# A two-layer SSD and S5 encoder on one core: other buffers, another PSUM tag and another order in the second layer

## The chip, the cores and the metric

The kernel runs on 1 core of one Trainium2 chip. A time is the device time of one execution in microseconds (us); of several runs the median is given. Durations and start times are read from the profile of one execution.

## What is computed

A trunk of two layers over 512 tokens of width 1024. The part that the change touches is the mixer:

```python
proj = h @ w_in
z = proj[..., :o1]
xbc = proj[..., o1:o2]
dt_raw = proj[..., o2:o3]
u = proj[..., o3:]
xbc = jax.nn.silu(depthwise_conv_centred(xbc, conv_w, conv_b))
...
y = y_fwd + y_bwd + ssd_d[:, None] * xh
y = y.reshape(bsz, l, SSD_WIDTH) * jax.nn.silu(z)
y_ssd = rms_norm(y, ssd_norm_w)
y5 = s5_bidirectional(u, ...)
g = jax.nn.gelu(y5)
y_s5 = rms_norm(g * jax.nn.sigmoid(g @ w_glu + b_glu), s5_norm_w)
return jnp.concatenate([y_ssd, y_s5], axis=-1) @ w_out
```

`y_fwd` and `y_bwd` are chunked state-space scans with 16 heads of 64 channels in 4 groups and a state of 128 (the SSD half); `s5_bidirectional` runs 64 groups of 16 channels through a complex diagonal state of 64, forward and backward (the S5 half). A layer norm follows, then `relu(h @ w1)**2 @ w2` and another layer norm.

## The kernel before

**Staging.** The layers run one after the other. Every product of activations with a weight is made as three fp32r matmuls (high part by high part, low by high, high by low: L105 to L107). For that ACT rounds each weight tile to its high part `whi` (L94) and DVE subtracts it to get `wlo` (L95); the raw tile is loaded by SP into one of two `raw` buffers.

**The mixer** of a layer consists of two generators. `s5_stream` makes the eight u tiles, then the V stage (L406, eight units, into the tile XV), then 62 steps of a scan on the 64 chunks, three DVE operations each (L423, L426, L427) and a copy back into XV by ACT (L428), then eight y units Y0 to Y7. A y unit loads its tables Gt, U and Wy through SP, multiplies them on PE (L527, L534) into one or two PSUM banks of the tag s5, and ACT takes them out with gelu (L539, tile gs). After every second unit PE transposes gs (L546, tile gT_ps), and the result goes to DRAM, to come back as gF for the glu product.

`ssd_group` runs four times. It makes the conv tiles B and C, and then for each of two head pairs (ct, 0 to 7 in all): the conv tile x (projection `xbc_ps`, L561 to L566), its transposition Xrow (L572), the products xd (L607), the states `st_ps` (L615) and S (L621, L630); then for each of the two heads the tile R (L653), the decay sums `D_ps` on PE (L661 to L664), their exponential E (L665), the weights w (L670 to L672), E times w (L674) and the tile eb (loaded by SP, multiplied at L675 and L676); then `y_ps` on PE (L685), the skip term (L694), the gate z (a projection, silu at L698, product at L699). Finished y tiles of the first three groups wait in DRAM.

**Order.** The table `KN["mrg"][l]` has 40 numbers, one for each step of `ssd_group` (10 for each group): so many steps of `s5_stream` are written ahead of that step. S5's step 13 ends the V stage, 44 the scan, 53 the last y unit. The list of instructions then goes through a scheduler, which orders each engine's queue by priority; `KN["po"][l]` shifts the priority of named pieces (a positive number is earlier): "yo" is y_ps, "y" the y units of S5, "cv" the conv tiles B and C, "wo" the output projection. Nothing in the code has the name "wp". Each engine then works through its queue in order.

**Buffers.** `KN["sb"][l]` gives the buffers of E, eb, R, w, tmp (w2 and z) and X (Xrow). PSUM has three banks of the tag mm, one of ss, two of sm and two of s5. `D_ps` has the tag sm, with `st_ps`, Xrow's, Brow's and others; v_ps, the y units and the glu product have s5.

**After both generators** the SSD half is finished: `rms_start` makes the tile ssq in the buffer of the tag "w"; `y_split` makes of each of the eight y tiles a high and a low part (L878, L879) and adds its squares to ssq (L710, L712, L714); `rms_ps` (L719) and r_ssd (L721) follow. Then half 0 of the output projection (`rp`, 192 matmuls on up to four accumulators; taken out at L907 with r_ssd), then glu, half 1, layer norm and MLP. In the order, half 0 is interleaved with the y units of S5.

Of the kernel before, what the change touches and what calls it, by code (L numbers as in the profile page):

```python
# [10 lines left out]
F32 = mybir.dt.float32  # L11
# [31 lines left out]
KN = dict(  # L43
    mrg=[[5, 0, 1, 0, 3, 6, 3, 5, 0, 5, 4, 3, 1, 0, 0, 0, 0, 0, 8, 0,
# [3 lines left out]
    pt0=3, lag=[1, 4], vb=(3, 2), gvb=(3, 2), cbb=2, wyb=4, raw=2, whi=3, wlo=3,  # L48
    nb=dict(mm=3, ss=1, sm=2, s5=2),
    po=[{"z": -100, "v": -30, "w": 150, "scan": -60, "R": -100, "y": -30, "dt": 300, "wp": 60, "wo": 30, "yo": 30}, {"w": -300, "dt": 300, "z": -150, "R": -30, "yo": 30, "wo": 30, "wp": 15, "cv": 100}],  # L50
    sb=[{"E": 3, "eb": 2, "R": 1, "w": 1, "tmp": 2, "X": 1}, {"E": 4, "eb": 4, "R": 1, "w": 1, "tmp": 3, "X": 2}],
    ybk=[1, 2], gt=["s5", "sm"], pwt=["sm", "sm"], stpe=[0, 0], curb=2, Dt="sm", gen="212002000222332121110000",
)


# [1 line left out]
def kernel(ctx: ExitStack, tc: tile.TileContext, A, out, depth=L):  # L57
    nc = tc.nc
    V, G, S, PE = nc.vector, nc.gpsimd, nc.scalar, nc.tensor
    per = ctx.enter_context(tc.tile_pool(name="per", bufs=1))  # L60
    wp = ctx.enter_context(tc.tile_pool(name="wp", bufs=3))
# [10 lines left out]
    def psum(tag, name, cols=512):  # L72
        return ps.tile([128, cols], F32, tag=tag, name=name, bufs=NB[tag], padded_shape=[128, 512])
# [504 lines left out]
    def ssd_group(l, pool, act, prm, dtp, g, yd, ys):  # L578
# [18 lines left out]
        for j in range(2):  # L597
# [3 lines left out]
            X, Xp = to_rows(pool, xT, "Xrow", KN["sb"][l]["X"])  # L601

            St = []
            for dd in range(2):
                c0 = dd
                xd = pool.tile([128, 3, 2, 64], F32, tag="xd", name="xd", bufs=1)
                V.tensor_tensor(xd, Xp[:, c0:c0 + 3].rearrange("p c (h q) -> p c h q", h=2),  # L607
                                dtp["dec"][:, c0:c0 + 3, dd, 2 * ct:2 * ct + 2].unsqueeze(3).to_broadcast([128, 3, 2, 64]),
                                op=ALU.mult)
                sp_ = psum("sm", "st_ps")  # L610
                order = [0, 1, 2] if dd == 0 else [2, 1, 0]
                on_pe = KN["stpe"][l]

                def state(i, alone):
                    PE.matmul(sp_[:, i * 128:(i + 1) * 128], lhsT=B[:, c0 + i],  # L615
                              rhs=xd[:, i].rearrange("p h q -> p (h q)"), start=True, stop=alone)
                for i in order:
                    if i == order[0] or not on_pe:
                        state(i, True)
                s_ = pool.tile([128, 3, 128], F32, tag="S", name="S", bufs=3)  # L620
                S.activation(s_[:, order[0]], sp_[:, order[0] * 128:order[0] * 128 + 128], AF.Copy)  # L621
                for a_, b_ in ((order[0], order[1]), (order[1], order[2])):
                    if on_pe:
                        ts = pool.tile([128, 128], F32, tag="ts", name="ts", bufs=2)
                    for h in range(2):
                        hs, tot = slice(h * 64, h * 64 + 64), dtp["tot"][:, b_ + dd, dd, 2 * ct + h:2 * ct + h + 1]
                        if on_pe:
                            S.activation(ts[:, hs], s_[:, a_, hs], AF.Copy, scale=tot)
                        else:
                            V.scalar_tensor_tensor(s_[:, b_, hs], s_[:, a_, hs], tot,  # L630
                                                   sp_[:, b_ * 128 + h * 64:b_ * 128 + h * 64 + 64],
                                                   op0=ALU.mult, op1=ALU.add)
                    if on_pe:
                        state(b_, False)
                        PE.matmul(sp_[:, b_ * 128:b_ * 128 + 128], lhsT=ident, rhs=ts, start=False, stop=True)
                        S.activation(s_[:, b_], sp_[:, b_ * 128:b_ * 128 + 128], AF.Copy)
                St.append(s_)
# [3 lines left out]
            for h in range(2):  # L641
                hh = 2 * ct + h
                E = pool.tile([128, T], F32, tag="E", name="E", bufs=KN["sb"][l]["E"])
                R = pool.tile([128, 2, 8, 64], F32R, tag="R", name="R", bufs=KN["sb"][l]["R"])
                eb = pool.tile([128, 2, 384], F32, tag="eb", name="eb", bufs=KN["sb"][l]["eb"])
# [5 lines left out]
                with prio("R"):  # L651
# [1 line left out]
                    V.tensor_tensor(R, cst[:, 384:512].rearrange("p (d t) -> p d t", d=2).unsqueeze(2).to_broadcast(  # L653
                        [128, 2, 8, 64]), av.rearrange("p x c d -> p d (x c)").bitcast(F32).unsqueeze(3).to_broadcast(
                        [128, 2, 8, 64]), op=ALU.mult)
                    Dp = psum(KN["Dt"], "D_ps")
                    Dv = Dp.rearrange("p (c t) -> p c t", c=4)
                    one = [av[:, x, :, d].unsqueeze(2).to_broadcast([128, 4, 64]) for x, d in ((1, 1), (0, 0))]
                    for x in range(2):
# [33 lines left out]
            y = xT  # L693
# [11 lines left out]
    def rms_start(pool, tag):  # L705
        return pool.tile([128, T], F32, tag=tag, name="ssq", bufs=1)
# [91 lines left out]
    for l in range(depth):  # L798
# [67 lines left out]
        with pool_("sd%d" % l) as pool:  # L866
# [4 lines left out]
                next(ssd, None)  # L871
            for _ in ssd:
                pass
            rms = rms_start(pool, "w")
            yT = new_hT()

            def y_split(k, y, first):
# [33 lines left out]
        with pool_("mo%d" % l, side="right") as pool:  # L911
            hT = new_hT()
            gb = load_gb(pool, 1 + 2 * l)
            with pool_("gl%d" % l, side="right") as gl:
# [9 lines left out]
                rms = rms_start(gl, "ssq")  # L924
# [174 lines left out]
```

## Time and profile before

| | us |
|---|---|
| median of 3 runs | 1854.35 |
| lowest and highest run | 1852.96, 1860.39 |
| the profiled execution | 1860.12 |
| its span in the profile | 1858.3 |
| PE busy | 1702.1 |
| DVE busy | 1269.6 |
| ACT busy | 762.8 |
| first V matmul of layer 2 (L406) | at 1048.0 |
| first scan step of layer 2 (L423) | at 1105.39 |
| first y matmul with Wy (L534) | at 1305.28 |
| first glu matmul | at 1398.85 |

Times in the lower part count from the start of the span. PE is TensorE's matmul queue, PEld its weight loads, which overlap; DVE is VectorE, ACT ScalarE, POOL GpSimd, SP the engine that issues most DMAs. PEclk is the granted clock of TensorE as a share of full speed. A wait is idle time of an engine and what ended it; "issue" is idle time for which the profile shows no releaser. Records of neighbouring matmuls overlap, so the pace of a chain of matmuls is the distance of their starts, not their duration.

### The profile page before, as it was taken

Reading aid. Unit: us, or ns where it says so; the run is one execution under the profiler, and the core shown is the slowest. Engines: PE = TensorE matmul, PEld = TensorE weight load, DVE = VectorE, ACT = ScalarE, POOL = GpSimd, SP = SyncE. Lnnn points to the kernel's source line nnn. Section 1 sums busy time; section 2 is a strip of 40 time slices with the busy share of each in tenths; the row PEclk is TensorE's granted clock in tenths of the full one; section 3 lists DMA queues with packets and bytes.
Section 4 is the critical chain, followed back from the end, with each engine's and each line's share of the span. In section 5 each row is a group of like instructions: output and inputs, shape, how many; then the busy total and the mean of one; then the engine's idle time right before and its main releaser. Section 6 shows DMA issues by size and latency. Waiting matters only on the chain.

```text
span 1858.3 us, 27757 instructions
## 1 busy us (share of the span) xinstructions
PE 1702.1 (92%) x11068; PEld 1384.9 (75%) x11068; DVE 1269.6 (68%) x2142; ACT 762.8 (41%) x1306; POOL 72.9 (4%) x101
## 2 busy tenths in 40 slices
PE   4999988769799999999999999886889999999998
PEld 3677766657578877777888887775677888888886
DVE  7579999996646989995347659999316663434346
ACT  3235557752144432323233556667315342313231
POOL 1000000000000101110001000000000000000001
PEclk9789989779899999999999999997899999999999
DMA  5767433144534287764334875230783323223232
GB/s 192 201 173 198 114 104 98 32 141 118 141 100 125 68 254 265 266 220 136 105 104 157 232 207 157 82 99 23 222 266 114 114 82 99 92 91 102 90 100 83
DMA packets 112049, 258.70 MB, mean 139 GB/s; under 512 B 10928, under 2 KB 54832, under 8 KB 111280
## 3 DMA queue, kind: packets, MB, share of 16 engines
q1 hardware_dynamic: 104432, 230.84, 41.4%
q0 software_dynamic: 7488, 26.09, 3.9%
q8 instruction: 87, 1.43, 0.3%
q14 instruction: 42, 0.34, 0.1%
HBM read 220.19 MB, written 36.70 MB: 138 GB/s over the span
## 4 chain that ended last, share of the span: by engine, by line
PE 69%; DVE 15%; DMA 8%; issue 4%; ACT 3%; SPq 0%; POOL 0%; POOLq 0%; DVEq 0%; ACTq 0%
PE rp L105 8%; PE rp L106 8%; PE rp L107 8%; PE up_ps L105 5%; PE up_ps L106 5%; PE up_ps L107 5%; PE xbc_ps L106 2%; PE xbc_ps L105 2%; PE xbc_ps L107 2%; PE v_ps L406 2%; DVE wlo L95 2%; PE y L534 2%; PE y_ps L685 2%; PE glu_ps L106 2%; PE glu_ps L105 2%
## 5 line engine op out<-in xcount | busy, mean ns | idle before, releaser
L95 DVE TENSOR_TENSOR wlo<-raw,whi 128x1024 fp32r<-128x1024 f32 x224 | 274.5, 1226 | 313.5 <-ACT whi L94 309.0
L94 ACT ACTIVATE whi<-raw 128x1024 fp32r<-128x1024 f32 x224 | 236.9, 1059 | 523.6 <-PE up_ps L106 170.0
L105 PE MATMUL up_ps<-hThi,whi 128*128 128x512 f32 (+1 forms) x560 | 208.1, 374 | 3.3 <-DVE hr L964 3.1
L106 PE MATMUL up_ps<-hTlo,whi 128*128 128x512 f32 (+1 forms) x560 | 208.6, 373 | 0.1
L107 PE MATMUL up_ps<-hThi,wlo 128*128 128x512 f32 (+1 forms) x560 | 208.2, 372 | 0.0
L106 PE MATMUL rp<-wlo,ahi 128*128 128x512 f32 x448 | 176.9, 395 | 0.4 <-DVE wlo L95 0.4
L107 PE MATMUL rp<-whi,alo 128*128 128x512 f32 x448 | 176.5, 395 | 0.0
L105 PE MATMUL rp<-whi,ahi 128*128 128x512 f32 x448 | 165.5, 397 | 1.6 <-ACT whi L94 1.6
L105 PEld LDWEIGHTS up_ps<-hThi,whi 128*128 128x128 f32 x560 | 105.0, 188 | 23.8 <-issue 2.4
L106 PEld LDWEIGHTS up_ps<-hTlo,whi 128*128 128x128 f32 x560 | 105.5, 188 | 18.8 <-issue 0.4
L107 PEld LDWEIGHTS up_ps<-hThi,wlo 128*128 128x128 f32 x560 | 105.5, 188 | 18.7 <-issue 0.4
L105 PE MATMUL xbc_ps<-hThi,whi 128*128 128x512 f32 x256 | 104.3, 413 | 7.6 <-ACT w L671 2.6
L106 PE MATMUL xbc_ps<-hTlo,whi 128*128 128x512 f32 x256 | 103.2, 409 | 0.0
L107 PE MATMUL xbc_ps<-hThi,wlo 128*128 128x512 f32 x256 | 103.1, 408 | 0.0
L105 PEld LDWEIGHTS rp<-whi,ahi 128*128 128x128 f32 x448 | 84.0, 188 | 22.5 <-ACT whi L94 2.5
L106 PEld LDWEIGHTS rp<-wlo,ahi 128*128 128x128 f32 x448 | 84.1, 188 | 20.8 <-DVE wlo L95 0.7
L107 PEld LDWEIGHTS rp<-whi,alo 128*128 128x128 f32 x448 | 84.1, 188 | 20.8 <-issue 0.2
L428 ACT ACTIVATE XV<-cur 128x128 f32<-128x128 f32 x124 | 52.4, 427 | 63.2 <-DVE cur L427 62.9
L974 DVE TENSOR_TENSOR h<-h,rp 128x512 f32<-128x512 f32 x64 | 43.8, 690 | 49.4 <-PE rp L107 49.4
L105 PE MATMUL u_ps<-hThi,whi 128*128 128x256 f32 (+1 forms) x176 | 61.0, 355 | 5.2 <-ACT whi L94 3.3
L685 PE MATMUL y_ps<-E,Xrow 128*64 128x128 f32 x256 | 49.6, 329 | 17.3 <-DVE E L674 17.3
L105 PEld LDWEIGHTS xbc_ps<-hThi,whi 128*128 128x128 f32 x256 | 49.8, 195 | 19.6 <-ACT z L698 3.2
(291 smaller groups left out, 3737.1 us busy)
## 6 DMA issues: line engine op xcount, KB each, us to landing
raw<-in_w SPq DMA_DIRECT2D x128, 512.0 KB, 3.6
raw<-in_wi SPq DMA_DIRECT2D x64, 512.0 KB, 3.7
Pv<-pd SPq DMA_DIRECT2D x32, 512.0 KB, 6.5
raw<-in_wo SPq DMA_DIRECT2D x32, 512.0 KB, 3.6
eb<-ad SPq DMA_DIRECT2D x64, 192.0 KB, 4.4
Bv<-in_bb SPq DMA_DIRECT2D x16, 512.0 KB, 5.7
U<-Ud SPq DMA_DIRECT2D x16, 512.0 KB, 5.9
Gt<-KKd SPq DMA_DIRECT2D x128, 64.0 KB, 3.1
```

The costliest lines, as they stand in the source:

```text
L94: S.activation(hi, raw, AF.Copy)
L95: V.tensor_tensor(lo, raw, hi.bitcast(F32), op=ALU.subtract)
L105: PE.matmul(o, lhsT=sh, rhs=mh, start=first, stop=False)
L106: PE.matmul(o, lhsT=sh, rhs=ml, start=False, stop=False)
L107: PE.matmul(o, lhsT=sl, rhs=mh, start=False, stop=last)
L406: PE.matmul(pv[64 * a:64 * a + 64, ri, q], lhsT=W[:, ri, g * 64:(g + 1) * 64], rhs=U[:, g, m % 2], start=True, stop=True, tile_position=(0 ...
L428: S.activation(x1, new, AF.Copy)
L534: PE.matmul(yv[b][64 * r:64 * r + 64, q], lhsT=XV[64 * a:64 * a + 64, ri, 4 * m + p, 64 * dd:64 * dd + 64], rhs=W[dd][64 * a:64 * a + 64, ...
L685: PE.matmul(yp[64 * h:64 * h + 64, c * 128:(c + 1) * 128], lhsT=lhsT[:, 64 * h:64 * h + 64], rhs=rhs[h], start=start, stop=stop, tile_posi ...
L974: V.tensor_tensor(hs, hs, o, op=ALU.add)
```

## The change

The entry of layer 2 (the second one) in four tables is new, E, eb and X get fewer buffers and R, w and xd more. `D_ps` of layer 2 takes its PSUM bank from the tag s5. In both layers ssq takes the buffer of the tag "CBU" (one of the two masked products of C and B, read at L670) instead of that of "w". The buffers of xd and S become entries of the table; for S and for layer 1 the numbers are those from before. No arithmetic is changed. The new table has one line more, so that each line of the changed kernel has a number one higher than here: L423 becomes L424, and so on.

```diff
--- before.py
+++ after.py
@@ -43,13 +43,14 @@
 KN = dict(
     mrg=[[5, 0, 1, 0, 3, 6, 3, 5, 0, 5, 4, 3, 1, 0, 0, 0, 0, 0, 8, 0,
           0, 1, 0, 0, 0, 0, 0, 0, 1, 0, 0, 0, 1, 1, 0, 0, 0, 2, 0, 2],
-         [3, 0, 2, 1, 0, 6, 9, 1, 5, 0, 0, 0, 0, 5, 0, 0, 0, 0, 1, 0,
-          0, 0, 1, 0, 0, 0, 0, 0, 2, 0, 3, 1, 0, 3, 0, 0, 1, 0, 0, 4]],
+         [3, 6, 3, 1, 0, 0, 4, 1, 5, 0, 5, 0, 3, 4, 1, 0, 0, 0, 1, 0,
+          0, 0, 0, 0, 0, 0, 0, 0, 2, 0, 3, 0, 1, 3, 0, 3, 0, 0, 0, 2]],
     pt0=3, lag=[1, 4], vb=(3, 2), gvb=(3, 2), cbb=2, wyb=4, raw=2, whi=3, wlo=3,
     nb=dict(mm=3, ss=1, sm=2, s5=2),
-    po=[{"z": -100, "v": -30, "w": 150, "scan": -60, "R": -100, "y": -30, "dt": 300, "wp": 60, "wo": 30, "yo": 30}, {"w": -300, "dt": 300, "z": -150, "R": -30, "yo": 30, "wo": 30, "wp": 15, "cv": 100}],
-    sb=[{"E": 3, "eb": 2, "R": 1, "w": 1, "tmp": 2, "X": 1}, {"E": 4, "eb": 4, "R": 1, "w": 1, "tmp": 3, "X": 2}],
-    ybk=[1, 2], gt=["s5", "sm"], pwt=["sm", "sm"], stpe=[0, 0], curb=2, Dt="sm", gen="212002000222332121110000",
+    po=[{"z": -100, "v": -30, "w": 150, "scan": -60, "R": -100, "y": -30, "dt": 300, "wp": 60, "wo": 30, "yo": 30}, {"w": -300, "dt": 300, "z": -150, "R": -30, "yo": -30, "wo": 30, "wp": 100, "cv": 100, "y": 150}],
+    sb=[{"E": 3, "eb": 2, "R": 1, "w": 1, "tmp": 2, "X": 1, "xd": 1, "S": 3}, {"E": 3, "eb": 2, "R": 2, "w": 2, "tmp": 3, "X": 1, "xd": 2, "S": 3}],
+    ybk=[1, 2], gt=["s5", "sm"], pwt=["sm", "sm"], stpe=[0, 0], curb=2, Dt=["sm", "s5"],
+    gen="212002000222332121110000",
 )
 
 
@@ -603,7 +604,7 @@
             St = []
             for dd in range(2):
                 c0 = dd
-                xd = pool.tile([128, 3, 2, 64], F32, tag="xd", name="xd", bufs=1)
+                xd = pool.tile([128, 3, 2, 64], F32, tag="xd", name="xd", bufs=KN["sb"][l]["xd"])
                 V.tensor_tensor(xd, Xp[:, c0:c0 + 3].rearrange("p c (h q) -> p c h q", h=2),
                                 dtp["dec"][:, c0:c0 + 3, dd, 2 * ct:2 * ct + 2].unsqueeze(3).to_broadcast([128, 3, 2, 64]),
                                 op=ALU.mult)
@@ -617,7 +618,7 @@
                 for i in order:
                     if i == order[0] or not on_pe:
                         state(i, True)
-                s_ = pool.tile([128, 3, 128], F32, tag="S", name="S", bufs=3)
+                s_ = pool.tile([128, 3, 128], F32, tag="S", name="S", bufs=KN["sb"][l]["S"])
                 S.activation(s_[:, order[0]], sp_[:, order[0] * 128:order[0] * 128 + 128], AF.Copy)
                 for a_, b_ in ((order[0], order[1]), (order[1], order[2])):
                     if on_pe:
@@ -653,7 +654,7 @@
                     V.tensor_tensor(R, cst[:, 384:512].rearrange("p (d t) -> p d t", d=2).unsqueeze(2).to_broadcast(
                         [128, 2, 8, 64]), av.rearrange("p x c d -> p d (x c)").bitcast(F32).unsqueeze(3).to_broadcast(
                         [128, 2, 8, 64]), op=ALU.mult)
-                    Dp = psum(KN["Dt"], "D_ps")
+                    Dp = psum(KN["Dt"][l], "D_ps")
                     Dv = Dp.rearrange("p (c t) -> p c t", c=4)
                     one = [av[:, x, :, d].unsqueeze(2).to_broadcast([128, 4, 64]) for x, d in ((1, 1), (0, 0))]
                     for x in range(2):
@@ -871,7 +872,7 @@
                 next(ssd, None)
             for _ in ssd:
                 pass
-            rms = rms_start(pool, "w")
+            rms = rms_start(pool, "CBU")
             yT = new_hT()
 
             def y_split(k, y, first):
```

The V stage of layer 2 is now written to its end by the fourth SSD step (before: by the seventh), and two or more y units lie before the last steps of the pairs 6 and 7. The rows below are the queues of single engines, in order, in layer 2's mixer.

DVE at the end of the scan (sc and cur are the scan's tiles, ssq the sum of squares of y). Before:

```order
L427 TENSOR_TENSOR cur<-sc_11576,sc_11575 128x128
L714 TENSOR_TENSOR ssq<-ssq,yl 128x512
L423 TENSOR_TENSOR sc_11694<-cur,l_5694 128x256
L714 TENSOR_TENSOR ssq<-ssq,yl 128x512
L426 TENSOR_TENSOR sc_11695<-sc_11694,XV 128x128
L427 TENSOR_TENSOR cur<-sc_11695,sc_11694 128x128
L423 TENSOR_TENSOR sc_11701<-cur,l_5694 128x256
L426 TENSOR_TENSOR sc_11702<-sc_11701,XV 128x128
L427 TENSOR_TENSOR cur<-sc_11702,sc_11701 128x128
L694 SCALAR_TENSOR_TENSOR xbc<-xbc,sp,y_ps 128x512
L879 SCALAR_TENSOR_TENSOR hTlo<-yl,sp,hThi 128x512 x2
L699 TENSOR_TENSOR xbc<-xbc,z 128x512
```

and with the change:

```order
L428 TENSOR_TENSOR cur<-sc_11583,sc_11582 128x128
L424 TENSOR_TENSOR sc_11589<-cur,l_5694 128x256
L427 TENSOR_TENSOR sc_11590<-sc_11589,XV 128x128
L428 TENSOR_TENSOR cur<-sc_11590,sc_11589 128x128
L654 TENSOR_TENSOR R<-cst,aT 128x1024
L675 TENSOR_TENSOR E<-E,w 128x512
L654 TENSOR_TENSOR R<-cst,aT 128x1024
L675 TENSOR_TENSOR E<-E,w 128x512
L673 TENSOR_TENSOR w<-w,w_12063 128x512
L673 TENSOR_TENSOR w<-w,w_12091 128x512
L713 COPY ssq<-yl 128x512
L715 TENSOR_TENSOR ssq<-ssq,yl 128x512 x3
```

The scan's last steps had ssq work between them, which now stands behind the scan, after R and E of the last two pairs.

ACT from the end of the scan to the second y unit (XV is the copy back of a scan step, gs the gelu of a y unit; y_11874 and y_11875 are the two halves of Y0 before, y_11616 and y_11617 those after, y_11750 and y_11751 Y1). Before:

```order
L428 ACTIVATE XV<-cur 128x64x2 x4
L878 ACTIVATE hThi<-yl,sp 128x512 x2
L428 ACTIVATE XV<-cur 128x64x2
L94 ACTIVATE whi<-raw 128x1024
L710 ACTIVATE yl<-yl 128x512 x2
L878 ACTIVATE hThi<-xbc,sp 128x512
L710 ACTIVATE xbc<-xbc 128x512
L94 ACTIVATE whi<-raw 128x1024
L539 ACT_TABLE_LOAD
L539 ACTIVATE gs<-y_11874 128x2x8x16
L539 ACTIVATE gs<-y_11875 128x2x8x16
L94 ACTIVATE whi<-raw 128x1024
```

and with the change:

```order
L429 ACTIVATE XV<-cur 128x64x2 x21
L540 ACT_TABLE_LOAD
L540 ACTIVATE gs<-y_11616 128x2x8x16
L540 ACTIVATE gs<-y_11617 128x2x8x16
L666 ACT_TABLE_LOAD
L666 ACTIVATE E<-D_ps 128x512 x2
L671 ACTIVATE w<-CBU,fac 128x128 x8
L699 ACT_TABLE_LOAD
L699 ACTIVATE z<-z_ps 128x512
L540 ACT_TABLE_LOAD
L540 ACTIVATE gs<-y_11750 128x2x8x16
L540 ACTIVATE gs<-y_11751 128x2x8x16
```

21 copies of the scan follow each other, and between gs of Y0 and gs of Y1 there are now E and w of a pair and z, with table loads.

PE from the last transposition of S5 (gT_ps) to the first glu matmuls. Before:

```order
L105 MATMUL rp_12621<-whi,hThi 128x512
L546 MATMUL gT_ps<-cst,gs 128x128 x8
L106 MATMUL rp_12621<-wlo,hThi 128x512
L107 MATMUL rp_12621<-whi,hTlo 128x512
L105 MATMUL rp_12621<-whi,hThi 128x512
L106 MATMUL rp_12621<-wlo,hThi 128x512
L107 MATMUL rp_12621<-whi,hTlo 128x512
L105 MATMUL glu_ps<-ahi,whi 128x512 x2
L106 MATMUL glu_ps<-alo,whi 128x512
L107 MATMUL glu_ps<-ahi,wlo 128x512
```

and with the change (between the two pieces stand 57 more rp matmuls):

```order
L106 MATMUL rp_12618<-whi,hThi 128x512
L547 MATMUL gT_ps<-cst,gs 128x128 x8
L107 MATMUL rp_12618<-wlo,hThi 128x512
L108 MATMUL rp_12618<-whi,hTlo 128x512
L106 MATMUL rp_12619<-whi,hThi 128x512
...
L106 MATMUL rp_12621<-whi,hThi 128x512
L107 MATMUL rp_12621<-wlo,hThi 128x512
L108 MATMUL rp_12621<-whi,hTlo 128x512
L106 MATMUL glu_ps<-ahi,whi 128x512
L107 MATMUL glu_ps<-alo,whi 128x512
L107 MATMUL rp_12618<-wlo,hThi 128x512
L108 MATMUL rp_12618<-whi,hTlo 128x512
```

Behind that transposition 5 rp matmuls stood before glu; now 62 do, and 24 more are mixed with glu's.

## Rows read from the trace of the kernel before

**Rows 1.** Page: engines' busy time and share; chain that ended last, by engine.
```profile
PE 1702.1 (92%) x11068; PEld 1384.9 (75%) x11068; DVE 1269.6 (68%) x2142; ACT 762.8 (41%) x1306; POOL 72.9 (4%) x101
...
PE 69%; DVE 15%; DMA 8%; issue 4%; ACT 3%; SPq 0%; POOL 0%; POOLq 0%; DVEq 0%; ACTq 0%
```

**Rows 2.** Windows: length, busy PE, PEld, DVE, ACT, POOL, then PEclk, DMA share, GB/s.
```profile
1050.00:1100.00 50.00, 48.85 (x585) 41.07 (x582) 24.59 (x40) 26.65 (x52) 1.77 (x2) 1.00 0.80 249
1150.00:1200.00 50.00, 43.53 (x239) 36.42 (x238) 48.38 (x106) 33.07 (x71) 0.00 (x0) 0.93 0.31 90
1250.00:1300.00 50.00, 34.60 (x226) 29.02 (x226) 46.36 (x108) 37.45 (x84) 0.00 (x0) 0.79 0.11 31
1350.00:1400.00 50.00, 44.21 (x450) 34.55 (x448) 11.23 (x13) 12.19 (x22) 1.62 (x3) 0.93 0.81 239
```

**Rows 3.** Groups on DVE, 1105 to 1304 us: busy us, mean ns, idle before.
```profile
L95 DVE TENSOR_TENSOR wlo<-raw,whi 128x1024 fp32r<-128x1024 f32 x17 | 20.7, 1218 | 0.0
...
L653 DVE TENSOR_TENSOR R<-cst,aT 128x1024 fp32r<-128x1024 f32 x13 | 15.9, 1220 | 0.7 <-PE D_ps L664 0.7
L630 DVE SCALAR_TENSOR_TENSOR S<-S,fac,st_ps 128x64 f32<-128x64 f32 x56 | 13.4, 278 | 0.3 <-ACT S L621 0.2
...
L714 DVE TENSOR_TENSOR ssq<-ssq,yl 128x512 f32<-128x512 f32 x3 | 2.0, 679 | 0.0
```

**Rows 4.** Waits of DVE, 1105 to 1304 us: total, times, longest.
```profile
DVE E L674 <- ACT E L665: 2.0, 3, 1.3
...
DVE eb L675 <- DMA eb<-ad: 0.5, 1, 0.5
```

**Rows 5.** Timeline of DVE, start and end of the scan: start, duration, line.
```profile
1105.39 0.41 DVE L423 TENSOR_TENSOR sc<-cur,l 128x256 f32<-128x256 f32 x1
...
1107.11 0.42 DVE L423 TENSOR_TENSOR sc<-cur,l 128x256 f32<-128x256 f32 x1
...
1108.31 0.43 DVE L423 TENSOR_TENSOR sc<-cur,l 128x256 f32<-128x256 f32 x1
...
1300.02 0.68 DVE L714 TENSOR_TENSOR ssq<-ssq,yl 128x512 f32<-128x512 f32 x1
1300.62 0.41 DVE L423 TENSOR_TENSOR sc<-cur,l 128x256 f32<-128x256 f32 x1
...
1303.30 0.29 DVE L427 TENSOR_TENSOR cur<-sc,sc 128x128 f32<-128x128 f32 x1
```

**Rows 6.** Windows, instructions of tile y_ps alone (columns: PE busy first, PEclk).
```profile
1258.00:1266.00 8.00, 2.40 (x38) 2.16 (x38) 0.00 (x0) 1.00 0.20 30
1294.00:1304.00 10.00, 4.93 (x40) 4.32 (x40) 0.49 (x1) 0.66 0.26 75
```

**Rows 7.** Waits of PE, 1304 to 1400 us: total, times, longest.
```profile
PE y L527 <- issue: 5.6, 1, 5.6
PE y L527 <- DMA Gt<-KKd: 3.5, 1, 3.5
...
PE y L527 <- DMA U<-Ud: 1.6, 1, 1.6
```

**Rows 8.** Line L539, whole span: duration min/median/max, first and last start.
```profile
L539 ACT ACTIVATE gs<-y x24: 365/384/602, 429.7 to 1391.8; 128x256 f32<-128x256 f32 x16, 128x512 f32<-128x512 f32 x8
L539 ACT ACT_TABLE_LOAD  x2: 1283/1283/1283, 424.7 to 1313.3; - x2
```

**Rows 9.** Timeline of PE: first L534, two rp, first glu.
```profile
1305.28 1.10 PE L534 MATMUL y<-Wy,XV 64*64 64x128 f32 x32 [2.30 <-issue]
...
1318.62 0.39 PE L107 MATMUL rp<-whi,hTlo 128*128 128x512 f32 x1
1318.85 0.40 PE L105 MATMUL rp<-whi,hThi 128*128 128x512 f32 x1
...
1398.85 0.73 PE L105 MATMUL glu_ps<-ahi,whi 128*128 128x512 f32 x2 [0.39 <-ACT ahi L921]
```

**Rows 10.** Page: DMA issues of eb; KB each, median us to landing.
```profile
eb<-ad SPq DMA_DIRECT2D x64, 192.0 KB, 4.4
```

## The prediction

> **What bounds the kernel now.** I read the engine table and the chain of the page first, then windows over layer 2's mixer, then the groups and waits of single engines in two stretches of it, then single rows. Over the whole span PE is busy 92% and carries 69% of the chain that ended last, DVE 15% [rows 1]: a change of order can only win time in which PE stands still or runs at a low clock. The windows show where that is. From 1050 to 1100 PE has 48.9 of 50 us busy; from 1150 to 1200 it has 43.5 and DVE 48.4; from 1250 to 1300 PE is down to 34.6, its granted clock to 0.79, and DVE still at 46.4 [rows 2]. The last two lie in the scan stage: the 62 scan steps (L423, L426, L427) run on DVE from 1105.39 to 1303.30 [rows 3, 5], 198 us, between the DVE work of the SSD pairs, and DVE waits in it for hardly anything (the largest wait is 2.0 us in all) [rows 4]. The first y unit of S5 needs the whole scan. After it PE is the busy one again (44.2 of 50 from 1350 to 1400) and DVE almost free (11.2) [rows 2]; this is the tail, from the first L534 at 1305.3 to the first glu matmul at 1398.9, 93.6 us [rows 9]. Its PE waits are few and long: 2.3 us ahead of the first L534 [rows 9], and before single L527 5.6 us of issue, 3.5 us for Gt and 1.6 us for U [rows 7], 13.0 us together.
>
> So three terms set what a new order of the same work does: when the scan can start (PE's V stage), how long DVE takes from its first to its last step, and how long PE takes from there to glu. Counted in the two orders, every engine issues the same compute work; only order, buffers and waits differ. Outside layer 2's mixer the orders are the same but for a few places at the end of layer 1's, which I count as nothing: the last scan step and the first y unit keep their places there.
>
> **Term 1, scan start.** Ahead of the last V unit the new order holds 20 y_ps, 12 D_ps and 4 projection matmuls fewer. A set of 20 y_ps took 2.40 us at clock 1.00 [rows 6]; a projection matmul starts every 0.23 us [rows 9], and a D_ps, with half the columns, I put at 0.114. That is 2.4 + 1.4 + 0.9 = 4.7 us less on a PE that is full there [rows 2]. The V weights then have to come in closer together, which can give some of it back; bounds 0 and -4.7, taken -4.
>
> **Term 2, the scan stage on DVE.** Between first L423 and last L427 the new order holds eight L630 fewer (0.278 us, 2.2), two L653 (1.22, 2.4), one L95 more (1.22) and, net, nine others of 512 columns or less fewer (L607, L672, L674, L694 and the like, with three conv ops more), which I take at the 0.68 of an L714 (6.1): -9.5 us [rows 3]. Neighbours that do not depend on each other overlap: the 0.68 us L714 that starts at 1300.02 is followed after 0.60, so each op costs 0.08 less than its duration; with 18 ops fewer that takes back 1.4. Ops that depend on each other do not overlap: a bare scan step takes 1.20 us (1107.11 to 1108.31), which is 0.04 us per op more than its durations [rows 5]. The new order has 22 more such neighbours (before ACT's 21 XV copies in a row DVE has nothing else to interleave), 22 x 0.12 = +2.6. So far -5.5.
> On top come waits that the trace of before cannot show, those for buffers. eb goes from four to two buffers. The next pair's eb can then be loaded only after y_ps of the last pair has read the old one, and a load takes 4.4 us from issue to landing [rows 10]. With four buffers DVE waited 0.5 us for it in the whole stage [rows 4]. By the new DVE order and the durations of this trace, the first eb product of the next pair stands 7.4, 5.9, 3.4, 1.7 and 2.6 us of DVE work behind the last pair's L694, which itself follows y_ps. If L694 came at once after y_ps, 1.0 + 2.7 + 1.8 = 5.5 us would be uncovered; if DVE's backlog keeps L694 2.7 us behind, nothing. Bounds 0 and +5.5, taken +1.5, as DVE is the late engine there. E from four to three and X from two to one are read by the same y_ps; the cover is the same backlog, and the term above holds them. R, w and xd go from one to two, which can only remove waits; DVE's largest is the 2.0 us for ACT's E, which these buffers do not touch [rows 4], so I take nothing for it. Term 2: -4 (bounds -7 and +1).
>
> **Term 3, the tail.** What was in front of the first y unit and now stands behind it on PE: D_ps (24) and y_ps (40) of pairs 6 and 7, six st_ps and four Xrow transposes. By rows 6 and the paces above 2 x 2.4 + 2.7 + 1.2 = 8.7 us. In return PE has even less to do at the end of the scan, where it was already down to clock 0.66 in the last ten microseconds [rows 6].
> How much of the 8.7 falls into the 13.0 us of waits [rows 7] is the open point. Three chains speak against all of it. **The banks:** layer 2's y units take both s5 banks, and D_ps now wants one of them, so D_ps of pair 6 waits for ACT to evacuate Y0 (0.38 us each, L539) [rows 8], and Y1 for the exponentials. **The tables:** ACT's order behind the scan now goes gelu, exp, silu, gelu, later exp, gelu: six table loads where there was one, 1.283 us each [rows 8], 6.4 us more on ACT, of which Y1 and Y4 stand behind some. **The accumulators:** wo half 0 (rp) cannot be evacuated before r_ssd, which needs all eight SSD tiles, and pair 7's now comes between Y5 and Y6 instead of before Y0; until then rp fills its four accumulators and stops. Walking PE's new order with these durations, the last y unit ends some 4 us sooner after Y0 than before, but 79 rp matmuls more are left behind it, 79 x 0.23 = 18 us. That makes the tail 14 us longer. If the waits stayed as they are it would be 8.7. I take +11, between the two. Bounds: all waits filled, 8.7 - 13.0 = -4.3; all of the 6.4 us of loads exposed, one y_ps set at the low clock (4.93 instead of 2.40 us [rows 6]) and 4 us for the banks, 8.7 + 13 = +22.
>
> A wait goes and another comes: the 5.6 us before an L527, which reads U and Gt, can be filled by pair 6's y_ps; late next is r_ssd. The rms sums move to the buffer of CBU, whose last reader now stands behind Y0; they are off PE's path until r_ssd, so nothing.
>
> **Sum:** -4 - 4 + 11 = +3 us. The profiled execution took 1860.1 us (span 1858.3), the longest of the three runs shown, 5.8 above the median of 1854.35; carried to the median this gives about 1857 us, and 0.5% (9.3 us), about what a measurement of this kernel can tell from no change, is not reached.
>
> The trace shows 1.283 us for a table load and nothing behind it that I would add [rows 8]. The Trainium skill, "ScalarE: Activation LUTs", section "What ACT_TABLE_LOAD costs", gives about 2.66 us for a switch, a drain included, and its section on table sets asks to batch calls by set, which speaks against this change; by it the five further loads are an estimated 13.3 instead of 6.4 us, and the sum would be up to 7 us higher if every one stood in PE's way.
>
> **The rivals.**
> *Faster: the holes take the work.* The tail's 13.0 us of waits are on DMAs (U, Gt), not on engines [rows 7]; pairs 6 and 7 bring 8.7 us of PE work that needs neither. If it all fits, the tail gets 4.3 us shorter, and with terms 1 and 2 the sum is -12, about 1842 us. For it: PE's order puts y_ps of pair 6 just ahead of Y2, where the 5.6 us were. Against: it needs Y0 evacuated and four activations in time. It decides where less than 3 us of PE waits are left. Chance 0.30 for a gain of over 0.5%.
> *Slower: PE waits for ACT between the y units.* One mechanism: D_ps in the s5 banks ties Y0, pair 6's exponentials and Y1 into one chain through ACT with its table loads, and again around Y4 with pair 7; rp, which could fill the gaps, has its accumulators full. At the upper bound, +22, the sum is +14, about 1868 us. It decides from 8.6 us more PE waiting in the tail than before. For it: ACT's order has exp and silu with eight w products between the gelus of Y0 and Y1. Against: before, ACT loaded the gelu table only at 1313.3, 8.0 us after Y0 began [rows 8, 9], so there is slack between the units. The rule of the Trainium skill named above would make this the likelier. Chance 0.27.
> *Nothing gained in the scan.* If eb and E with fewer buffers stop DVE for 5 us, terms 1 and 2 shrink to -4 and the sum goes to +7, 1861 us: within the forecast's bounds, so it has no chance of its own.
> *The change does not act* where scan start and tail are ruled by the Wv and U loads, which stay; then 1854. This and the forecast share 0.43.
>
> The likeliest single case is the forecast of no measurable change. The range reaches down to the full holes with term 1 at its bound (-16, 1838) and up to the slower rival with some of term 2 lost (1872), and leaves out 2 in 10.
>
> **What would show it.** In the changed trace: the last V matmul some 4 us earlier; first to last scan op about 194 us instead of 198, with DVE's waits for eb under 2 us; the first y matmul about 1297; PE idle just before it, with a clock under 0.8; from there to glu about 105 us instead of 93.6, less if PE's waits between the y units are under 3 us, more if D_ps or y waits for ACT's E or gs for over 8 us. I would be wrong if the scan stage got longer (eb or E waits on DVE), or if the tail stayed at 94 us or less.

## The result and the profile after

The changed kernel took 1880.31 us, the median of 9 runs (1864.16 to 1889.68); the kernel before 1860.39 in 9 runs beside them (1850.67 to 1865.19). The ratio is 1.0105, 95% interval 1.0078 to 1.0133: slower, by some 20 us (14 to 25). The prediction had no measurable change, 1857 us within 1838 to 1872; the time lies outside that range.

The page of the changed kernel, its engine table and the chain by engine, for [rows 1]:

```profile
PE 1706.1 (91%) x11068; PEld 1382.1 (74%) x11068; DVE 1272.8 (68%) x2142; ACT 761.4 (41%) x1304; POOL 72.6 (4%) x101
...
PE 69%; DVE 13%; DMA 7%; issue 6%; ACT 3%; SPq 1%; POOL 0%; POOLq 0%; DVEq 0%; ACTq 0%
```

The busy times are those of before within 4 us, and the span is 20 us longer (1878.5 after 1858.3): PE stands still longer. The same four windows as in [rows 2], of the changed kernel:

```profile
1050.00:1100.00 50.00, 50.00 (x608) 41.62 (x607) 22.90 (x28) 26.04 (x50) 1.77 (x2) 1.00 0.83 264
...
1150.00:1200.00 50.00, 49.36 (x288) 40.26 (x289) 46.12 (x90) 31.91 (x71) 0.00 (x0) 1.00 0.36 105
...
1250.00:1300.00 50.00, 28.97 (x175) 23.47 (x173) 45.15 (x112) 27.77 (x67) 0.00 (x0) 0.83 0.20 58
...
1350.00:1400.00 50.00, 46.40 (x578) 36.87 (x577) 14.34 (x24) 17.58 (x29) 3.21 (x5) 1.00 0.79 262
```

PE is fuller while the V stage and the first pairs run, and emptier at the end of the scan (29.0 of 50 against 34.6). To see where the 20 us are, layer 2's mixer is cut at its own events: first u matmul, first scan step, end of the scan; first y matmul, first glu, end of glu. Windows of the kernel before (columns: length, busy PE, PEld, DVE, ACT, POOL, then PEclk, DMA share, GB/s):

```profile
1002.10:1105.40 103.30, 102.04 (x1114) 88.28 (x1114) 55.25 (x97) 51.62 (x89) 5.49 (x7) 1.00 0.73 221
1105.40:1303.60 198.20, 168.08 (x990) 140.93 (x989) 188.90 (x417) 134.46 (x286) 0.00 (x0) 0.91 0.34 97
1305.30:1398.80 93.50, 81.70 (x864) 64.44 (x864) 22.08 (x26) 24.18 (x41) 4.37 (x7) 0.91 0.76 233
1398.80:1446.40 47.60, 45.72 (x193) 36.23 (x194) 31.91 (x38) 25.91 (x37) 0.00 (x0) 1.00 0.39 119
```

and of the changed kernel:

```profile
1010.50:1107.90 97.40, 96.77 (x1061) 83.75 (x1061) 49.35 (x87) 45.94 (x80) 5.50 (x7) 1.00 0.69 217
1107.90:1311.00 203.10, 162.69 (x923) 130.52 (x921) 183.96 (x398) 123.69 (x270) 0.00 (x0) 0.90 0.33 96
1311.50:1416.00 104.50, 89.08 (x960) 71.27 (x961) 40.61 (x60) 42.36 (x71) 4.32 (x7) 0.91 0.73 233
1416.00:1466.60 50.60, 50.60 (x218) 40.79 (x217) 30.39 (x34) 23.58 (x31) 0.00 (x0) 1.00 0.32 98
```

From first u to scan start -5.9 us, scan +4.9, tail +11.0, glu +3.0; with 1.2 us less between scan and first y, +11.8 in all. Most of it is PE standing still: in the scan stage PE is idle for 40.4 us after 30.1, in the tail for 15.4 after 11.8. The rest lies ahead of the mixer: the changed kernel starts it 8.4 us later. In layer 1, the rows of the first y matmuls and of the first glu matmul (first and last start after the durations), before:

```profile
L534 PE MATMUL y<-Wy,XV x512: 269/269/473, 424.4 to 523.4; 64*64 64x128 f32 x171
L105 PE MATMUL glu_ps<-ahi,whi x64: 392/397/500, 526.2 to 571.9; 128*128 128x512 f32 x64
```

and after:

```profile
L535 PE MATMUL y<-Wy,XV x512: 269/269/473, 427.0 to 531.3; 64*64 64x128 f32 x171
L106 PE MATMUL glu_ps<-ahi,whi x64: 392/397/501, 534.1 to 579.8; 128*128 128x512 f32 x64
```

From the first y to the first glu it is 101.8 us before and 107.1 after: +5.3, in the layer whose table was not touched.

### The profile page after: what moved, and what is told of

Its sections match the earlier page's. It is cut to its first block, busy times and chain, and to the rows that moved or that the text cites. A ratio compares the mean times of both kernels' runs of the same rounds, so it can differ in the third digit from the quotient of the medians.

```text
span 1878.5 us, 27764 instructions
## 1 busy us (share of the span) xinstructions
PE 1706.1 (91%) x11068; PEld 1382.1 (74%) x11068; DVE 1272.8 (68%) x2142; ACT 761.4 (41%) x1304; POOL 72.6 (4%) x101
## 4 chain that ended last, share of the span: by engine, by line
PE 69%; DVE 13%; DMA 7%; issue 6%; ACT 3%; SPq 1%; POOL 0%; POOLq 0%; DVEq 0%; ACTq 0%
PE rp L107 8%; PE rp L108 8%; PE rp L106 8%; PE up_ps L106 5%; PE up_ps L107 5%; PE up_ps L108 5%; PE xbc_ps L106 3%; PE xbc_ps L107 2%; PE xbc_ps L108 2%; PE v_ps L407 2%; DVE wlo L96 2%; PE glu_ps L107 2%; PE glu_ps L106 2%; PE glu_ps L108 2%; PE y_ps L686 1%
## 5 line engine op out<-in xcount | busy, mean ns | idle before, releaser
L535 PE MATMUL y<-Wy,XV 64*64 64x128 f32 x1024 | 63.6, 306 | 32.5 <-issue 32.5
L535 PEld LDWEIGHTS y<-Wy,XV 64*64 64x64 f32 x1024 | 49.8, 151 | 43.1 <-issue 43.1
```

The source lines that it names most:

```text
L535: PE.matmul(yv[b][64 * r:64 * r + 64, q], lhsT=XV[64 * a:64 * a + 64, ri, 4 * m + p, 64 * dd:64 * dd + 64], rhs=W[dd][64 * a:64 * a + 64, ...
```

## The experiments

Theory A: three costs, layer 1's ssq in another buffer (5 us), DVE's waits for eb and X with fewer buffers in layer 2's scan stage, and what the new table puts behind the first y unit. Rivals: chance between executions (B), the s5 tag of D_ps (C), the order itself as the cause of DVE's waits (D), DVE's work between V and the first y as what sets the end in any order (E). Each change of a buffer or tag also moves the order, so the expectations name what the order of each kernel has behind the first y unit, Y0. The three kernels that add one piece to before (eb, the table, the priorities) also have layer 2's ssq in the buffer of CBU, which their diffs do not show, so their layer 2 is compared with the run that moves only ssq. "V stage", "scan", "tail" and "glu" are the windows of above, the V stage from the first u matmul to the first scan step (the expectations count it to the last V matmul, some 2 us less); the mixer is from the first u matmul to the last glu matmul.

**Layer 1's ssq back, layer 2 as in the change.**

```diff
-            rms = rms_start(pool, "CBU")
+            rms = rms_start(pool, "CBU" if l else "w")
```

> The change with layer 1's ssq back in the buffer of w, so that layer 1 is as before and layer 2 as in the change. Theory A (the moved ssq costs layer 1 its 8 us): the stretch from layer 1's first y matmul to its first glu matmul falls from 107.1 to 101.8 us, the time from about 1880 to 1872. Rival B (layer 1's 8 us are a difference between two executions): the stretch and the time stay within 3 us of the change's. Layer 2's stages stay in both: scan about 203, first y matmul to glu about 104.5.

Ratio to before 1.0100 (1.0066 to 1.0135). Layer 1's stretch is 102.2 us (first y at 417.4, first glu at 519.6); layer 2 repeats the change's to 0.6 us in every stage (scan 203.7, tail 104.5, glu 50.6). The median, 1877.14, is only 3 us below the change's, and the interval is too wide to tell 5 us from none; the stretch shows it.

**The other way round: before, with only ssq moved.**

```diff
-            rms = rms_start(pool, "w")
+            rms = rms_start(pool, "CBU")
```

> The kernel before with nothing changed but the buffer of ssq (that of CBU instead of w), in both layers. Theory A (the moved ssq costs layer 1 some 5 us): the stretch from layer 1's first y matmul to its first glu is about 107 us, as in the four traces with CBU (106.4 to 107.9), and not 102, as in the two with w. Rival B (chance): about 102. Layer 2 in both: within 3 us of before.

Its two rows:

```profile
L534 PE MATMUL y<-Wy,XV x512: 269/269/473, 418.8 to 522.0; 64*64 64x128 f32 x171
L105 PE MATMUL glu_ps<-ahi,whi x64: 392/397/501, 524.8 to 570.5; 128*128 128x512 f32 x64
```

106.0 us. Over all profiles of this study the stretch is 106.0 to 107.9 us in the five with CBU in layer 1 and 101.5 to 102.5 in the nine with w: no overlap, so not chance. What the traces add: with CBU one weight split for rp comes on DVE 14 us after the first y instead of 26, and from the second y unit on DVE's table work for Wy runs some 3 us later (its longest wait for a cb load 6.3 us instead of 3.7). Which of the two holds up the other was not tried. Layer 2: the mixer is 443.4 against 444.3, but the scan stage is 203.2 and the tail 86.6, so of the 3 us expected only the sum holds.

**How far a stage repeats: before, unchanged, a second profile.**

> The kernel before unchanged, for a second profile: how far the stages repeat. If the differences told apart here are not chance, layer 1's stretch from first y to first glu is 102 within 1 us, and of layer 2 the scan stage 198, the tail 93.5 and the mixer 444 within 2 us.

```profile
1004.30:1108.10 103.80, 102.04 (x1114) 88.23 (x1114) 55.91 (x98) 51.73 (x89) 5.50 (x7) 1.00 0.73 219
1108.10:1311.70 203.60, 172.58 (x990) 144.28 (x989) 189.10 (x417) 134.54 (x286) 0.00 (x0) 0.88 0.34 95
1313.20:1403.90 90.70, 78.24 (x865) 61.43 (x865) 22.19 (x26) 24.38 (x41) 4.38 (x7) 0.96 0.77 240
```

Layer 1 repeats (102.2). The scan stage does not: 203.6 instead of 198.2 at the same DVE work, with a lower clock (0.88), and the tail gives 2.8 of it back. So the scan stage of before is 198 to 204, and the +4.9 of the first comparison is not shown to be the change's. The mixer, 444.3 and 447.2, repeats to 3 us; the change's, 456.1 and 456.2, stands 9 to 12 above it. PE's idle time in the scan stage repeats better than the stage: 30.1 and 31.0 us before (33.5 with only ssq moved), 40.4 and 41.2 in the two profiles of the changed mixer.

**Layer 2's buffers back.**

```diff
-"E": 3, "eb": 2, "R": 2, "w": 2, "tmp": 3, "X": 1, "xd": 2, "S": 3
+"E": 4, "eb": 4, "R": 1, "w": 1, "tmp": 3, "X": 2, "xd": 1, "S": 3
```

> The change with layer 2's buffers back (E 4, eb 4, X 2, R, w and xd 1); table, priorities and tag as in the change. Theory A (DVE's 20 us of waits in the scan stage come from eb and X with fewer buffers): waits of DVE for eb and for xd fall from 8 to under 2 us, the scan stage from 203 to about 195, the time by about 8 us. Rival D (the waits come from the order, R and w with one buffer take over): the scan stage stays above 200.

Ratio 1.0192 (1.0159 to 1.0224): slower than the change. Waits for eb 2.9 us, for ACT's w 3.3, scan stage 206.5, tail 117.2. As rival D had it; with this table the old buffers are worse, not better.

**eb alone, on the kernel before.**

```diff
-"E": 4, "eb": 4, "R": 1
+"E": 4, "eb": 2, "R": 1
```

> The kernel before with eb of layer 2 at two buffers instead of four and layer 2's ssq in the buffer of CBU; layer 1 as before. Theory A (eb at two buffers stops DVE): DVE's waits for eb's loads in the scan stage rise from 0.5 us to 3 us or more, the scan stage from 198 to 201 or more. Rival D (DVE's backlog hides the load, the waits in the change come from its order): the waits for eb stay under 1.5 us and the scan stage within 2 us of 198.

DVE's largest waits in its scan stage:

```profile
DVE eb L677 <- DMA eb<-ad: 4.5, 4, 2.0
DVE R L654 <- PE D_ps L665: 2.0, 1, 2.0
DVE eb L676 <- DMA eb<-ad: 1.6, 4, 0.8
```

6.1 us for eb, where before's two profiles and that with only ssq moved have 0.5, 2.5 and 1.5. So two buffers do cost DVE some 4 to 6 us of waits. The scan stage, 205.6, is 2.4 above the run with only ssq moved; but the tail is 97.2 us instead of 86.6 and the mixer 459.6 instead of 443.4. With the order that goes with it, eb at two buffers lengthens the mixer of before by 16 us in this one profile, more than the waits account for.

**eb at three buffers, on the change with layer 1 as before.**

```diff
-"E": 3, "eb": 2, "R": 2
+"E": 3, "eb": 3, "R": 2
```

> The change with layer 1 as before and eb of layer 2 at three buffers instead of two; its order has the same work on either side of Y0. Theory F (of the 10 us of new idle time of DVE in the scan stage the eb buffers cause 3 to 4): waits for eb from 4.0 to 5.4 us down to under 1.5, the scan stage from 203 to about 199.5. Rival D (eb waits come from the order of SP's queue, not from the buffers): the waits for eb stay above 3 us.

Waits for eb's loads 2.7 us instead of 4.0 and 5.4 (not under 1.5), scan stage 200.3 instead of 203.7: -3.4, the size that theory F had, but less than before's two profiles differ by. The tail is 112.5 instead of 104.5, with a wait of 9.2 us of PE's gT_ps for ACT's gs in it that the change does not have, and a clock of 0.87 instead of 0.92. What the scan stage may have gained is given back.

**D_ps back in sm.**

```diff
-Dt=["sm", "s5"]
+Dt=["sm", "sm"]
```

> The change with D_ps of layer 2 back in the PSUM tag sm; the order moves with it: only pair 7 (12 D_ps, 20 y_ps) is left behind Y0 instead of pairs 6 and 7, with three table loads instead of six, and 82 dependent neighbours in the scan stage instead of 101. Theory A (what stands behind Y0 is paid in the tail): the tail falls from 104.5 to about 98 (one pair, 4.4 us, and three loads less), the scan stage gets some 8 us longer as pair 6's DVE work is back in it, in all -6 to +2 us. Rival C (the s5 tag itself makes the tail long): the tail falls to 94 or less and the time by 10 us or more.

Ratio 1.0175 (1.0135 to 1.0216), slower than the change with intervals that just do not meet, where theory A had -6 to +2 us. Tail 100.9 (-3.6 for one pair, where theory A had -6.5), scan 216.3, 13 us more. Rival C falls.

**The new table alone, on before.**

```diff
-         [3, 0, 2, 1, 0, 6, 9, 1, 5, 0, 0, 0, 0, 5, 0, 0, 0, 0, 1, 0,
-          0, 0, 1, 0, 0, 0, 0, 0, 2, 0, 3, 1, 0, 3, 0, 0, 1, 0, 0, 4]],
+         [3, 6, 3, 1, 0, 0, 4, 1, 5, 0, 5, 0, 3, 4, 1, 0, 0, 0, 1, 0,
+          0, 0, 0, 0, 0, 0, 0, 0, 2, 0, 3, 0, 1, 3, 0, 3, 0, 0, 0, 2]],
```

> The kernel before with the new merge table of layer 2 alone (and layer 2's ssq in the buffer of CBU); priorities, buffers and tag as before, layer 1 as before. Its order has one pair's D_ps and y_ps behind Y0 and 168 rp ahead of glu, 24 mixed with it. Theory A (the table is what makes the tail long): V stage 5 us earlier, tail from 93.5 to about 102, glu 3 us longer; in all +5 to +15 us against before. Rival C (the tag and the buffers are the cost, the table a gain): no slower than before, -5 us or better.

Ratio 1.0138 (1.0099 to 1.0178), some 26 us slower than before, where theory A had 5 to 15. V stage 97.1 us, scan 203.3, tail 119.9, glu 50.6. In the mixer (471.4) the table by itself costs more than all of the change (456); the intervals of the times overlap.

**The old table in the change.**

```diff
-         [3, 6, 3, 1, 0, 0, 4, 1, 5, 0, 5, 0, 3, 4, 1, 0, 0, 0, 1, 0,
-          0, 0, 0, 0, 0, 0, 0, 0, 2, 0, 3, 0, 1, 3, 0, 3, 0, 0, 0, 2]],
+         [3, 0, 2, 1, 0, 6, 9, 1, 5, 0, 0, 0, 0, 5, 0, 0, 0, 0, 1, 0,
+          0, 0, 1, 0, 0, 0, 0, 0, 2, 0, 3, 1, 0, 3, 0, 0, 1, 0, 0, 4]],
```

> The change with layer 2's old merge table; buffers, tag and priorities as in the change. By its order nothing of pairs 6 and 7 is left behind Y0 and only 96 rp matmuls are, with one table load; in the scan stage DVE has 429 operations instead of 397. Theory A (the merge table made the tail long): the tail falls from 104.5 to about 80 as half of rp stands ahead of Y0, the scan stage grows by 15 us or more, in all between -12 and 0 us against the change. Rival C (the s5 tag of D_ps makes the tail long whatever the table): the tail stays above 95 and the time is no better than the change's.

Ratio 1.0092 (1.0057 to 1.0126). Tail 81.8 and scan 216.2, near theory A; but the V stage is 109.2 us, 6 more than in before, and the mixer, 453.8, is only 2 us shorter than the change's. So without the new table the other pieces still cost nearly as much.

**The new priorities alone, on before.**

```diff
-"yo": 30, "wo": 30, "wp": 15, "cv": 100
+"yo": -30, "wo": 30, "wp": 100, "cv": 100, "y": 150
```

> The kernel before with the new priorities of layer 2 alone (yo -30, y 150; layer 2's ssq in the buffer of CBU); table, buffers, tag and layer 1 as before. Its order has 128 rp behind Y0 instead of 192 and 427 DVE operations in the scan stage instead of 415. Theory A: the tail gets shorter by some 12 us (64 rp fewer are 14.6 us of PE), the scan stage longer by some 8 us, in all -5 to +5 us against before. If the holes of the scan stage take the 64 rp at no cost to DVE, it is the version that beats both, by up to 12 us.

Ratio 1.0049 (1.0018 to 1.0081). Scan 212.6, tail 86.3, mixer 455.0. Against the run with only ssq moved (203.2, 86.6 and 443.4) the tail gains nothing and the scan stage is 9 us longer; theory A had 12 us less in the tail. It is slower than before by some 9 us.

**The change with pairs 6 and 7 in front of Y0.** Layer 1 is as before. Of the change in layer 2, the first thirty numbers of the table, buffers, tag and priorities stay; in the second run the priorities are before's too.

```diff
-          0, 0, 0, 0, 0, 0, 0, 0, 2, 0, 3, 0, 1, 3, 0, 3, 0, 0, 0, 2]],
+          0, 0, 0, 0, 0, 0, 0, 0, 2, 0, 3, 0, 0, 1, 0, 0, 1, 0, 0, 4]],
```

> The change with layer 1 as before and the last ten numbers of layer 2's merge table as 3 0 0 1 0 0 1 0 0 4, so that the S5 steps of the y units come after pair 7; the first thirty numbers, buffers, tag and priorities as in the change. By its order nothing of pairs 6 and 7 stands behind Y0, and 96 rp do; DVE has 442 operations in the scan stage instead of 397. Theory A (what stands behind Y0 is paid in full in the tail, and the early V stage is a gain): V stage 95 us as in the change, tail from 104.5 to about 82, scan stage from 203 to about 217, glu 3 to 4 us shorter; the mixer 9 to 15 us shorter than the change's 456, so level with before (444) or a little better. Rival E (the gain of the early V stage is lost again in any order, since DVE's work between V and Y0 sets the end): the scan stage is 225 or more and the mixer no better than the change's.

> The same with layer 2's priorities as before as well, so that of the change only the first thirty numbers of the table, the buffers and the tag are left. Its order has the same work on either side of Y0, with 84 dependent neighbours in the scan stage instead of 90. Theory A: as the run above within 3 us, so that the priorities are not what counts. A rival by which the priorities matter: 5 us or more apart.

Ratios 1.0041 (1.0011 to 1.0070) and 1.0065 (1.0035 to 1.0094). Windows of the first, cut as above (first u to scan start, scan, tail):

```profile
1001.90:1099.10 97.20, 96.79 (x1062) 83.77 (x1062) 49.24 (x87) 45.95 (x80) 5.50 (x7) 1.00 0.69 218
1099.10:1329.90 230.80, 196.96 (x1139) 159.97 (x1137) 211.29 (x443) 145.22 (x303) 0.00 (x0) 0.93 0.38 111
1330.50:1411.30 80.80, 61.62 (x769) 47.85 (x769) 10.92 (x14) 15.80 (x31) 4.38 (x7) 0.87 0.73 230
```

The tail is 23.7 us shorter than the change's, and the scan stage 27.7 longer than it: 27.3 us of DVE work went in (211.3 after 184.0), and all of it shows in the stage. The mixer is 455.3, no better than the change's 456, as rival E had it for this order. By its time the kernel is nearer to before than the change with layer 1 as before is (1.0100), with intervals that just overlap; the single profile does not show why. Between these two kernels the priorities count for little (mixers 455.3 and 456.9).

None of the eight that were timed in six or more runs beats the kernel before; the other four have one run each. Side by side, in us, from one profile each where not two are given:

| kernel | V stage | scan | tail | mixer |
|---|---|---|---|---|
| before, two profiles | 103.3, 103.8 | 198.2, 203.6 | 93.5, 90.7 | 444.3, 447.2 |
| before, ssq moved | 103.6 | 203.2 | 86.6 | 443.4 |
| before, ssq moved, new priorities | 103.6 | 212.6 | 86.3 | 455.0 |
| before, ssq moved, eb at two buffers | 105.7 | 205.6 | 97.2 | 459.6 |
| before, ssq moved, new table | 97.1 | 203.3 | 119.9 | 471.4 |
| the change, layer 1's ssq moved and not | 97.4, 96.9 | 203.1, 203.7 | 104.5, 104.5 | 456.1, 456.2 |
| the change, old table | 109.2 | 216.2 | 81.8 | 453.8 |
| the change, D_ps in sm | 98.1 | 216.3 | 100.9 | 468.6 |
| the change, old buffers | 97.7 | 206.5 | 117.2 | 472.6 |
| the change, pairs 6 and 7 in front | 97.2 | 230.8 | 80.8 | 455.3 |

Each of the three pieces put into before by itself makes the mixer longer by 12 to 28 us, and taking the table, the tag or the buffers out of the change gives back some 2 us at most. No single piece is the cost; the tag alone was not put into before.

## Why the prediction was wrong

Three steps failed: the waits of term 2, taken as 1.5 us; term 3, too small by 3 to 6 us; and layer 1, counted as nothing, where 5.3 us were lost.

**Term 1 was right in kind.** Predicted -4 (bounds 0 to -4.7): first u to scan start got 5.9 us shorter, a little more than the bound, and it is 96.9 to 98.1 us in all eight kernels with the first thirty numbers of the new table, against 103.3 and 103.8 in before's two profiles.

**But it was no gain, and that was not seen.** DVE did 5.9 us less work in that stretch (49.35 after 55.25): the DVE work of what PE left behind the V stage went into the scan stage, where DVE is busy for over 90% of the time. From first u to the end of the scan DVE's busy time fell by 10.9 us (244.2 to 233.3), all of it work that now stands behind Y0; the length fell by 1.0 us against before's first profile (301.5 to 300.5) and by 6.9 against its second (307.4). Terms 1 and 2 together had -8.

**Term 2 failed in its waits.** "Taken +1.5" was the step. DVE's busy time in the scan stage fell by 4.9 us (188.9 to 184.0), near the 5.5 of the text. Its idle time rose from 9.3 us (14.5 in the second profile of before) to 19.1. The largest waits of the changed kernel, for [rows 4]:

```profile
DVE R L654 <- PE D_ps L665: 3.6, 2, 2.9
DVE eb L676 <- DMA eb<-ad: 2.5, 3, 1.4
DVE E L675 <- ACT E L666: 1.7, 2, 1.1
DVE eb L677 <- DMA eb<-ad: 1.5, 3, 1.0
DVE xbc L695 <- PE y_ps L686: 1.4, 1, 1.4
```

eb's share, 4.0 us after 0.5 (2.5 in before's second profile), is inside the bounds I gave for it (0 to 5.5) but over the value taken. The others I had at nothing: R, for which "can only remove waits" was said, has 3.6 us (2.8 in the second profile of the changed mixer, 0.7 and 2.4 in before's). A likely reason, not tried by itself: with fewer pairs' work in the stage DVE has less to go on with when one pair's D_ps or y_ps is late. Also a bare scan step took 1.27 us at the end of the scan, not 1.20:

```profile
1308.46 0.42 DVE L424 TENSOR_TENSOR sc<-cur,l 128x256 f32<-128x256 f32 x1
...
1309.73 0.42 DVE L424 TENSOR_TENSOR sc<-cur,l 128x256 f32<-128x256 f32 x1
```

So the predicted -4 became +4.9 against one profile of before and -0.5 against the other.

**Term 3 was right in sign and mis-sized by 3 to 6 us.** Predicted +11: first y to first glu grew by 11.0 (13.8 against before's second profile). But I had put the 24 rp that are mixed with glu into the tail's count; they came on top, 3.0 us in the glu stretch: +14, the value that the walk through PE's order gave and that I cut. That it came out to the microsecond is luck, as that walk had no term for the loads. The holes did not take the work. PE's stops of over 1 us in the tail of the change, for [rows 7, 9]:

```profile
1311.51 1.99 PE L535 MATMUL y<-Wy,XV 64*64 64x128 f32 x32 [32.54 <-issue]
...
1335.54 1.12 PE L528 MATMUL y<-Gt,U 128*64 128x128 f32 x8 [7.10 <-issue]
...
1344.62 1.65 PE L106 MATMUL rp<-whi,hThi 128*128 128x512 f32 x3 [3.36 <-ACT whi L95]
...
1365.68 0.66 PE L528 MATMUL y<-Gt,U 128*64 128x128 f32 x8 [1.14 <-DMA U<-Ud]
...
1385.62 0.62 PE L528 MATMUL y<-Gt,U 128*64 128x128 f32 x7 [1.61 <-DMA U<-Ud]
```

The wait of 5.6 us before an L527 is there again, with 7.1: pair 6's y_ps stands ahead of it and did not fill it. The 3.4 us for whi are new: ACT had just waited 8.8 us for the load of yl, and then 0.7 us for the weight itself. Both loads left late, and no term had that. SP works through its queue in order too, and there stood, ahead of them, the loads of Gt for a later y unit. Gt has two buffers, so these waited until Y0 was done with one. SP's largest wait from 1270 to 1420 us:

```profile
SPq L516 <- PE y L528: 53.6, 4, 43.5
```

For 43.5 us, to 1314.6, SP issued nothing; eb, yl and the first weight for rp followed from 1329.4 to 1332.3. So the first rp matmul starts 33.1 us behind the first y; before, the first two weights were issued at 1301.7, ahead of the Gt of a later unit, and rp starts 4.0 us behind the first y. Ahead of the first y PE had nothing for 32.5 us, the bare end of the scan. Before, work of pairs 6 and 7 stood there.

**The slower rival's mechanism did not happen.** PE waited for ACT's E and gs between the y units for about 0.5 us each, and its idle time in the tail grew by 3.6 us where the rival asked for 8.6. (With eb at three buffers one wait for gs took 9.2 us, so the mechanism can appear in a near order.) All six table loads are there (three L540, two L666, one L699, 1283 ns each). Between gs of Y0 and gs of Y1 they lie in ACT's chain, but PE had the matmuls of Y1 and of pair 6 to do meanwhile. One switch, with the end of z ahead of it and gs behind it:

```profile
1324.15 0.60 ACT L699 ACTIVATE z<-z_ps 128x512 f32<-128x512 f32 x1
1324.76 1.28 ACT L540 ACT_TABLE_LOAD   x1
1326.06 0.66 ACT L540 ACTIVATE gs<-y 128x256 f32<-128x256 f32 x2
```

From z's end to gs it is 1.3 us, the load alone. By the Trainium skill, "ScalarE: Activation LUTs", section "What ACT_TABLE_LOAD costs", the five further switches would have been an estimated 13.3 us (about 2.66 us each, a drain included). The trace agrees on the load, 1283 ns, but shows no drain behind it, and PE paid for little of either. The time came out on the rival's side for other reasons.

**What no term had is layer 1.** "Which I count as nothing: the last scan step and the first y unit keep their places there" was wrong by 5.3 us. The move of ssq to another buffer changed some places of rp and of one weight split, behind the first y unit, where I had not looked.

The sum, as it was: -5.9 + 4.9 - 1.2 + 11.0 + 3.0 in the mixer and +5.3 in layer 1, 17.1 us, with 3 us more that lie elsewhere in layer 1 and that single profiles cannot tell from chance (the stretch up to the end of layer 1's V stage alone varies from 188 to 200 us between profiles). Of the 23 us between the forecast of 1857 and 1880.31 some 6 are the base and not the change: the forecast took the profiled 1860.1 for 5.8 above the median, but it is near the median of nine runs, 1860.39. (The low end of the range, -16, needs term 2 at its bound as well as term 1: -4.7 - 7 - 4.3.)

**What stays open.** Which pieces of the change work against which in layer 2 is not shown: the table alone costs most, but with the old table in the change the mixer is only 2 us shorter, as more work stands in its V and scan stages. Why the tail is 104.5 us in one order and 112 to 120 in others with nearly the same work behind Y0 is not settled either. Their clocks are 0.86 to 0.87 against 0.91 and 0.92. The first rp matmul comes 33 us behind the first y in both profiles with 104.5, 56 us with 117.2 and 78 us with 119.9, but 28 us with 112.5, so that is not all of it. No run moved SP's loads by themselves.

## What to carry to other kernels

Where one engine fills a stage (here DVE the scan), starting the stage earlier can merely pull work into it that stood ahead: count that engine's work from a fixed point before the stage to its end, not the stage's start. Work that was moved across the end of that stage was paid on either side: 27.3 us of DVE work put back into it made it 27.7 us longer and the tail 23.7 shorter. Look also at what the queue that issues the loads waits for: here one load that needed a late buffer held up the loads behind it for 43.5 us. A change of a buffer's tag moves the order wherever the tag is used; compare the orders of every part of the program that has it, and not only of the one that the change is about.

## What the runs showed that I had not expected

Two profiles of one kernel differ by 5 us in a stage that one engine fills to 93 to 95%, and give half of it back in the next; a stage's time from one profile is no better than that. Layer 1's stretch of 102 us, by contrast, repeats to 1 us over nine profiles.
